# Residual rows of the output projection over five places, and two weight splits of the memory traced two steps later

## The chip, the cores and the metric

The kernel runs on one core of one Trainium2 chip. The metric is the device time in microseconds of one execution. A second kind of execution is taken by the hardware profiler, and all views of the profile below come from that one. The engines are TensorE (PE, with its weight loads shown apart as PEld), VectorE (DVE), ScalarE (ACT), GpSimd (POOL) and SyncE (SP), on whose queue all transfers of this kernel are issued.

## The reference

One inference step of one layer of a streaming encoder, for a prompt of 1024 frames and a sample of 64 frames that share the weights, in f32. Cut to what matters:

```python
h = rms_norm(xp, g_norm1)
qa, ka, va, qb, kb, vb, logf = in_proj(h, w_in, b_f, g_qa, g_ka, g_qb, g_kb)
oa = chunk_band_attn_prompt(qa, ka, va, rel_bias)   # 8 heads, 64-frame chunks, 8 chunks back
ob = forget_attn_prompt(qb, kb, vb, logf)           # 8 heads, causal, with forget bias
xp = xp + concat([oa, ob]) @ w_o                    # output projection and residual
mk, mv = mem_kv(mem_prompt, g_mem, w_mkv, g_mk)     # keys and values of 256 memory tokens
xp = xp + mem_attend(rms_norm(xp, g_norm2), mk, mv, w_mq, g_mq, w_mo)
xp = xp + conv_ffn(rms_norm(xp, g_norm3), zeros, w_up, w_conv, b_conv, w_down)
```

The sample goes through the same with cached keys and values. The outputs are both streams and the new keys, values, forget logits and conv states.

## The kernel before, in words

Every f32 product is made of three products of a high and a low part (`SPLIT = ((0, 0), (0, 1), (1, 0))`): an operand `raw` is split into `hi`, its rounded copy, made by ScalarE, and `lo = raw - hi`, made by VectorE or GpSimd. Activations are kept transposed, in 8 tiles of 128 features by 1088 frames (1024 of the prompt and 64 of the sample). The frames are worked on in three chunks of 384, 384 and 320 columns (`CHUNKS`).

The stages in order of time: projection and attention by head pairs (up to about 600 us in the profile), the memory's keys and values together with the sample's attention (to about 700), the output projection (to about 815), the memory's attention, and the feed-forward part.

The program is traced as Python. A planner then orders each engine's instructions when the program is compiled. Where the code wants an order kept it says so, as with `tc.keep_in_program_order(mm)` for the first matmul of the memory's keys. So the place in the trace of the program ranks an instruction, and the order in which it runs can differ. Waits between engines, and for a tile's place to be free, are put in by the framework: a tile tag with `bufs=n` has n places in turn.

*Around the splits.* After the last head pair is projected, its attention remains, and runs in four steps, `LEFT = (0, 0, 0, 15)`: each step traces the pieces of attention that are due (`substeps()`), and the number says how many pieces of the memory's product (`line`) are woven in. An attention piece goes through the bias (POOL, L485, with the causal mask L486), the score matmuls into the one bank S (L499), the masked maximum (DVE, L502), the exponential (ACT, L504), the scaling by the sum (L507 and L509), transposes into the banks PT (L539), their split into `pth` (ACT, L540) and `ptl` (DVE, L541), the value sum into the one bank O (L554), and its end: a copy `otmp` (ACT, L563) and an add into `mix` (DVE, L564).

The memory's weights come in 8 slices n of 256 columns. Each slice has two loads `mwraw` (`load_wm`, L661, two places) and four splits (`split_wm`, y = 0 to 3, two for each load): a cast `mwhi` on ACT (L668) and a subtraction `mwlo` (L669), on GpSimd for even y and on VectorE for odd y. Slice 0 has its splits y = 0 and 1 traced ahead of the four steps and y = 2 and 3 in the first pieces of `line`, in the fourth step. `load_mem` loads the memory tokens and splits them (`mhi` on ACT, L265, `mlo` on DVE, L266). The memory's matmuls are L679.

*The output projection.* `project` goes through 24 products (feature tile m, chunk c). For each it loads the residual chunk from `xT` (L1066) into the first half of a row tile, adds the product to it into the second half (DVE, L1073), stores that to `x1d` (L1074), and makes from it the next operand (`hhi`, ACT, L1076; `hlo`, DVE, L1077) and its square (ACT, L1079 or L1082), which GpSimd adds to one accumulator for each chunk (L1083). `after_o` reduces the accumulators over the features on PE (L1098). The row tile is the tag `qhi`, which has two places; `qlo` has two and `pth`, `ptl` and `sq` one each:

```python
BUFS = {"qhi": 2, "qlo": 2, "kvraw": 2, "s": 3}
```

The same tags serve the memory's attention afterwards: `qhi`, `qlo` and `sq` in `Mem.query`, `pth` and `ptl` in `Mem.turn`. The products go to two banks `PT` for the third and fourth and to two banks `pj` for the others; w_o's parts come through `Stream` (loads `raw`, L911; `hi`, ACT, L919; `lo`, POOL, L920).

## Time and profile before

| | |
|---|---|
| timed runs | 1780.97, 1782.76, 1785.41 us; median 1782.76 |
| profiled execution, its own time | 1788.58 us |
| its span, first to last instruction | 1786.6 us |
| mean granted TensorE clock | 0.988 |
| PE busy | 1717.5 us, 96% |
| DVE, ACT, POOL busy | 1210.5, 941.2, 647.3 us |
| DMA | 199.87 MB, mean 112 GB/s |

Times in the views are microseconds from the span's start. A row of a timeline gives the start, the duration, engine, line, operation, output and inputs with shapes, how many instructions are merged in it, and in brackets how long the engine stood idle before and what ended that. A row of waits gives the total, the number and the longest. A row by stretches gives the stretch, its length, the busy time and number of instructions of each engine, the granted clock as a share of the full one, the busy share of the DMA engines and GB/s.

### The profile page before, as it was taken

The page shows a single profiled execution, that of the slowest core. Times are in us where ns is not written, and L with a number is a line of the kernel's source. Part 1 is how long each engine was busy: PE and PEld are TensorE (multiplying, and loading weights), DVE is VectorE, ACT ScalarE, POOL GpSimd, SP SyncE. Part 2 cuts the span into 40 slices and gives each one's busy share as a digit, 9 for nine tenths or more (in the row PEclk, how much of TensorE's full clock was granted, in tenths as well). Part 3 has the DMA queues.
Part 4 walks back from the last instruction along what each step waited for, and adds up shares of the span by engine and source line. Part 5 has one row for each costly group of instructions (what it writes and reads, how often), then busy time and mean ns, then how long its engine had stood idle before and what let it go on. Part 6 is the DMA issues. An engine that isn't in the chain of part 4 may idle for free.

```text
span 1786.6 us, 33930 instructions
## 1 busy us (share of the span) xinstructions
PE 1717.5 (96%) x12432; PEld 1668.3 (93%) x12432; DVE 1210.5 (68%) x2643; ACT 941.2 (53%) x2058; POOL 647.3 (36%) x931
## 2 busy tenths in 40 slices
PE   7898999999998898999999999999999999999999
PEld 6888999999997777999999999999999999999999
DVE  5768667677677686433444369877777777649986
ACT  6756667677677577433555456434333333434432
POOL 4556667778777443453443612100000000000000
PEclk8999999999999999999999999999999999999999
DMA  7322222122112777541111563222222222693332
GB/s 251 91 62 64 60 77 78 49 74 76 51 56 83 216 252 219 165 143 56 54 54 60 151 214 104 79 75 77 79 85 85 85 73 73 216 346 130 118 104 88
DMA packets 134391, 199.87 MB, mean 112 GB/s; under 512 B 20984, under 2 KB 74360, under 8 KB 134224
## 3 DMA queue, kind: packets, MB, share of 16 engines
q1 hardware_dynamic: 134224, 197.70, 35.0%
q8 instruction: 98, 1.61, 0.4%
q14 instruction: 69, 0.57, 0.1%
HBM read 155.35 MB, written 45.44 MB: 112 GB/s over the span
## 4 chain that ended last, share of the span: by engine, by line
PE 46%; DVE 4%; issue 2%; ACT 1%; POOL 1%; DMA 1%; SPq 0%; DVEq 0%; ACTq 0%; POOLq 0%
PE W L1449 24%; PE W L1773 11%; PE pj L937 7%; PE S L1192 1%; PE tq L1228 1%; PE O L1228 1%; POOL lo L920 1%; DVE f L1314 0%; PE PT L1215 0%; DMA f<-x2d 0%; DVE lo L920 0%; DMA h<-ad 0%; PE O L1192 0%; ACT hi L1313 0%; DVE qhi L1301 0%
## 5 line engine op out<-in xcount | busy, mean ns | idle before, releaser
L299 PE MATMUL pj<-whi,xhi 128*128 128x384 f32 (+1 forms) x512 | 195.8, 382 | 2.7 <-DVE flog L314 1.6
L299 PE MATMUL pj<-wlo,xhi 128*128 128x384 f32 (+1 forms) x512 | 177.0, 346 | 4.3 <-POOL wlo L123 4.3
L299 PE MATMUL pj<-whi,xlo 128*128 128x384 f32 (+1 forms) x512 | 175.9, 344 | 0.7 <-DVE xlo L131 0.7
L1555 POOL COPY s<-gp 128x2 f32<-128x2 f32 x22 | 15.8, 720 | 335.8 <-DVE gp L1554 335.8
L1449 PE MATMUL W<-h,hi 128*128 128x272 f32 x704 | 134.4, 288 | 1.4 <-ACT qlo L1585 1.4
L504 ACT ACTIVATE s<-s,mx 128x640 f32<-128x640 f32 (+7 forms) x128 | 94.4, 737 | 77.4 <-DVE mx L502 76.5
L1773 PE MATMUL W<-f,hi 128*128 128x272 f32 x672 | 127.1, 287 | 0.1
L541 DVE TENSOR_TENSOR ptl<-PT,pth 128x512 fp32r<-128x512 f32 (+2 forms) x192 | 99.4, 522 | 37.5 <-ACT pth L540 35.3
L1449 PEld LDWEIGHTS W<-h,hi 128*128 128x128 f32 x704 | 110.8, 188 | 1.6 <-ACT qlo L1585 1.6
L540 ACT CAST pth<-PT 128x512 fp32r<-128x512 f32 (+2 forms) x192 | 84.7, 449 | 41.7 <-PE PT L539 39.9
L1773 PEld LDWEIGHTS W<-f,hi 128*128 128x128 f32 x672 | 105.3, 188 | 0.4 <-DVE f L1520 0.4
L299 PEld LDWEIGHTS pj<-wlo,xhi 128*128 128x128 f32 x512 | 99.5, 194 | 5.9 <-POOL wlo L123 5.9
L299 PEld LDWEIGHTS pj<-whi,xhi 128*128 128x128 f32 x512 | 99.4, 194 | 4.3 <-DVE flog L314 1.9
L1449 PE MATMUL W<-h,lo 128*128 128x272 f32 x352 | 101.8, 289 | 0.0
L299 PEld LDWEIGHTS pj<-whi,xlo 128*128 128x128 f32 x512 | 98.3, 192 | 1.4 <-DVE xlo L131 1.2
L1773 PE MATMUL W<-f,lo 128*128 128x272 f32 x336 | 96.7, 288 | 0.0
L539 PE MATMUL PT<-ident,s 128*128 128x128 f32 x528 | 89.9, 277 | 6.9 <-DVE ptl L541 5.4
L1313 ACT CAST hi<-raw 128x512 fp32r<-128x512 f32 x68 | 42.2, 621 | 98.6 <-PE W L1449 59.2
L499 PE MATMUL S<-kh,q 128*128 128x256 f32 (+1 forms) x304 | 77.8, 281 | 13.5 <-DVE mx L502 13.5
L937 PE MATMUL pj<-a,hi 128*128 128x384 f32 (+1 forms) x352 | 89.3, 337 | 0.2 <-DMA mraw<-mixd 0.2
L507 POOL TENSOR_SCALAR s<-s,ssum 128x640 f32<-128x640 f32 (+6 forms) x96 | 70.8, 738 | 47.9 <-DVE ssum L505 34.3
L554 PE MATMUL O<-pth,v 128*128 128x256 f32 (+1 forms) x304 | 76.5, 277 | 8.5 <-DVE mix L564 7.7
(538 smaller groups left out, 6037.6 us busy)
## 6 DMA issues: line engine op xcount, KB each, us to landing
raw<-in_w_down_dram SPq DMA_DIRECT2D x45, 256.0 KB, 2.8
wraw<-in_w_dram SPq DMA_DIRECT2D x56, 192.0 KB, 2.5
raw<-in_w_up_dram SPq DMA_DIRECT2D x41, 256.0 KB, 2.8
h<-ad SPq DMA_DIRECT2D x32, 272.0 KB, 5.5
mwraw<-in_w_mkv_dram SPq DMA_DIRECT2D x16, 512.0 KB, 6.1
raw<-in_w_mo_dram SPq DMA_DIRECT2D x32, 256.0 KB, 3.2
kvraw<-in_w_down_dram SPq DMA_DIRECT2D x32, 256.0 KB, 3.0
ad<-t SPq DMA_DIRECT2D x22, 272.0 KB, 2.2
```

Source lines behind the costliest of these rows:

```text
L299: pe.matmul(pj[:, :nw], x2[a][:, k, t * P:(t + 1) * P], wt[k][b][:, :nw], start=n == 0, stop=n == 3 * KT - 1)
L499: pe.matmul(sp[:, a:a + (k1 - k0) * P], q, kk[:, h, src], start=m == 0, stop=m == 1)
L504: act.activation(s[:, :n], s[:, :n], ACT.Exp, bias=mx, scale=-1.0, accum_out=sm)
L507: pool.tensor_scalar(s[:, :n], s[:, :n], sm, 1.0, op0=ALU.mult, op1=ALU.mult)
L539: pe.transpose(pt[:, b - ch[0]], self.s[j][:, (b - w0) * P:(b - w0 + 1) * P], ident)
L540: act.copy(hi[:, f:f + n, j], pt[:, f:f + n])
L541: dve.tensor_tensor(lo[:, f:f + n, j], pt[:, f:f + n], f32(hi[:, f:f + n, j]), op=ALU.subtract)
L554: pe.matmul(op[:, cols], groups[p, b // 2].v[:, b % 2, h].rearrange("p a d -> p (a d)"), pt[:, x, cols], start=b == self.full[0] and m == ...
L937: pe.matmul(out()[:, :cn], w[a][:, k % 4], x[b][k][:, c0:c0 + cn], start=k == 0 and n == 0, stop=k == KT - 1 and n == 2)
L1313: act.copy(hi, t)
L1449: pe.matmul(w[:, z, :Q], a(p, j), rights[j][b][:, z * Q:z * Q + Q], start=fresh and begin and j == 0 and x == 0, stop=final and end and j ...
L1773: pe.matmul(ws[m][:, z, :Q], la[p][:, m * P:(m + 1) * P], ra[b][:, z * Q:z * Q + Q], start=first and y == 0 and what in opening, stop=fina ...
```

## The change

Two edits. The two splits y = 0 and 1 of the memory's slice 0 (the first two quarters of its weights) are traced at the start of the third step in place of ahead of the first. And the residual row of product n takes its place from a list of five in turn: `qhi`, `pth`, `qhi`, `ptl`, `sq`, of which `qhi` has two places.

```diff
     load_mem(0)
     load_wm(0, 1)
     load_mem(1)
-    split_wm(0, 0)
-    split_wm(0, 1)
-    for n in LEFT:
+    for x, n in enumerate(LEFT):
+        if x == 2:
+            split_wm(0, 0)
+            split_wm(0, 1)
         step(n, substeps())
...
         for n, (m, c) in enumerate(order):
             c0, cn = CHUNKS[c]
-            xr = row("qhi", 768)
+            xr = row(("qhi", "pth", "qhi", "ptl", "sq")[n % 5], 768)
             xr, xo = xr[:, 0:cn], xr[:, 384:384 + cn]
             if firsts and n == 0:
                 xr = early_x
```

## The prediction

> **What bounds the kernel now.** I read the page's head first, then the busy time by stretches around the two places that the diff touches.

> ```profile
> PE 1717.5 (96%) x12432; PEld 1668.3 (93%) x12432; DVE 1210.5 (68%) x2643; ACT 941.2 (53%) x2058; POOL 647.3 (36%) x931
> ```

> TensorE works 96% of the span, so time is won only where TensorE waits or runs slowly. The second view says how the touched places stand in that.

> ```profile
> 565.00:575.00 10.00, 6.02 (x48) 5.52 (x46) 6.83 (x17) 7.66 (x20) 4.10 (x8) 0.95 0.65 210
> 575.00:585.00 10.00, 4.73 (x19) 3.88 (x19) 8.38 (x12) 7.22 (x15) 7.27 (x10) 0.54 0.73 246
> 585.00:600.00 15.00, 11.82 (x85) 10.02 (x86) 10.88 (x23) 10.49 (x19) 8.54 (x10) 1.00 0.72 204
> ...
> 720.00:740.00 20.00, 20.00 (x122) 19.57 (x121) 7.26 (x21) 7.59 (x18) 6.87 (x6) 1.00 0.55 167
> ```

> The columns after the stretch are its length, then busy time and instructions of PE, PEld, DVE, ACT and POOL, then the granted clock. From 565 to 600, where the attention of the last head pair ends and the memory's weights come in, PE is idle for 4.0 + 5.3 + 3.2 = 12.5 us, and has half a clock in the middle. The output projection, from 720 on, has PE busy without a hole. These are the places of the two halves of the change.

> **The moved splits.** The list of PE's waits between 560 and 705 us has this at its head:

> ```profile
> PE O L554 <- DVE mix L564: 7.7, 1, 7.7
> ```

> The value sum of the attention needs the one bank named O, which is free when ScalarE has copied it (otmp, L563) and VectorE has added it (mix, L564). Here is what stood around these two: ScalarE, VectorE, GpSimd, the DMA queue (with the landing times of the raw weights), and PE:

> ```profile
> 571.77 1.29 ACT L265 ACTIVATE mhi<-s,gcol 128x256 fp32r<-128x256 f32 x3
> 574.31 1.14 ACT L668 CAST mwhi<-mwraw 128x512 fp32r<-128x512 f32 x2 [1.24 <-DMA mwraw<-in_w_mkv_dram]
> 575.47 0.37 ACT L563 COPY otmp<-O 64x256 f32<-64x256 f32 x1
> 575.86 1.07 ACT L540 CAST pth<-PT 128x512 fp32r<-128x512 f32 x2
> 576.82 1.15 ACT L668 CAST mwhi<-mwraw 128x512 fp32r<-128x512 f32 x2
> ```
> ```profile
> 575.48 3.00 DVE L669 TENSOR_TENSOR mwlo<-mwraw,mwhi 128x512 fp32r<-128x512 f32 x1 [1.89 <-ACT mwhi L668]
> 578.51 0.42 DVE L564 TENSOR_TENSOR mix<-O,otmp 64x256 f32<-64x256 f32 x1
> 578.85 1.07 DVE L502 CUSTOM_DVE_ANT_0 s<-S,s 128x896 f32<-128x896 f32 x1
> ...
> 585.58 1.29 DVE L669 TENSOR_TENSOR mwlo<-mwraw,mwhi 128x512 fp32r<-128x512 f32 x1
> ...
> 587.87 0.83 DVE L669 TENSOR_TENSOR mwlo<-mwraw,mwhi 128x512 fp32r<-128x512 f32 x1
> ```
> ```profile
> 575.69 1.01 POOL L485 TENSOR_SCALAR s<-bias,ctok 128x896 f32<-128x896 f32 x1
> 576.66 1.26 POOL L669 TENSOR_TENSOR mwlo<-mwraw,mwhi 128x512 fp32r<-128x512 f32 x1
> 577.89 0.74 POOL L486 TENSOR_SCALAR_AFFINE_SELECT s<-s 128x128 f32<-128x128 f32 x1
> ...
> 583.57 0.29 POOL L486 TENSOR_SCALAR_AFFINE_SELECT s<-s 128x128 f32<-128x128 f32 x1
> ```
> ```profile
> 578.54 0.34 SPq L661 DMA_DIRECT2D mwraw<-in_w_mkv_dram  x1
> ```
> ```profile
> DMA to landing us min/median/max: 3.6/6.1/8.8
> ```
> ```profile
> 579.07 0.55 PE L554 MATMUL O<-pth,v 128*128 128x256 f32 x1 [7.69 <-DVE mix L564]
> 579.98 0.58 PE L499 MATMUL S<-kh,q 128*128 128x256 f32 x1 [0.36 <-DVE mx L502]
> ```

> The change moves two splits, y0 and y1: two casts on ScalarE (574.31), y0's subtraction on GpSimd (576.66) and y1's on VectorE (575.48). They issue no DMA themselves, but the end of y1 frees a raw buffer, and the next load on the SP queue stands right behind it (575.48 + 3.00 = 578.48, issue at 578.54); that load moves too. Without the two casts, otmp goes when the three mhi end, at 571.77 + 1.29 = 573.06; with 0.37 for it, 0.42 for mix and the 0.14 from mix's end to the matmul as now (578.93 to 579.07), the O matmul runs at 574.0, 5.1 us earlier.

> That is not yet 5.1 us of time. PE executes in order, and behind that matmul stand the scores (579.98), which wait for the one S bank, read by the maximum L502 (578.85). L502 needs the bias from GpSimd: L485 ends at 575.69 + 1.01 = 576.70, and the masking L486, no longer behind y0, takes 0.29 in its short row: 577.0. So L502 starts at 577.0 in place of 578.85: **1.85 us gained** on the path. The rest of the 5.1 us turns into a new wait, for L502.

> What is late next: the moved work must go somewhere. ScalarE has 10 - 7.22 = 2.8 us idle in the stretch 575 to 585 for the casts (1.14), GpSimd 2.7 us for y0 (1.26); both are hidden there and would cost those durations if L504's exponentials or the biases stood behind them. On VectorE I expect y1 beside y3, the split of lowest rank, which now runs at 585.58 between two L502 whose results free the S bank. VectorE does not idle there (no idle mark in either row), and I charge the row of y3, **1.29 us**; the ends are 0.83 and 3.00, and 1.29 is the nearest in place. But then the next raw load goes out near 586.9 and lands at least 3.6 us later, past 590, so that the subtraction of the following quarter, at 587.87, leaves the full part too: **0.83 us back**. Sum of this half: -1.85 + 1.29 - 0.83 = **-1.39 us**; its ends are -5.1 (nothing else holds the path) and +0.3 (-1.85 + 3.00 - 0.83).

> [...]

> **The rotated rows.** Before, each residual chunk is loaded, added to and stored from one of two places, so load n+2 waits until store n has landed. Five places take that wait away. No instruction is added or removed: 23 loads and 24 stores stay on SP, the loads earlier, and the weights' loads behind them on that queue are held up less. What do the waits cost now? From VectorE three adds of the stage, then PE where it comes nearest to waiting, then PE's waits from 705 to 830 us:

> ```profile
> 737.00 0.49 DVE L1073 TENSOR_TENSOR qhi<-PT,qhi 128x320 f32<-128x320 f32 x1 [3.71 <-DMA qhi<-in_xT_dram]
> ...
> 739.48 0.56 DVE L1073 TENSOR_TENSOR qhi<-pj,qhi 128x384 f32<-128x384 f32 x1 [0.80 <-DMA qhi<-in_xT_dram]
> ...
> 804.30 0.56 DVE L1073 TENSOR_TENSOR qhi<-pj,qhi 128x384 f32<-128x384 f32 x1 [2.00 <-PE pj L937]
> ```
> ```profile
> 740.21 0.56 PE L937 MATMUL pj<-a,hi 128*128 128x384 f32 x2
> ```
> ```profile
> PE pj L937 <- POOL lo L920: 0.7, 1, 0.7
> PE PT L1098 <- POOL kSl L1083: 0.6, 1, 0.6
> ```

> The early adds wait up to 3.71 us for a load; the late ones wait for PE itself. Neither stops PE: two banks PT and two pj take the products meanwhile. It is close: the product that starts at 740.21 reuses the bank of the add of 739.48, which ends at 740.04. So the waits are hidden, narrowly, and taking them away gives **0**; without that cover each would cost PE its own length. The wait of 0.6 at the stage's end follows a sum behind a PE product, not a load. The ends are -0.6, should earlier sums clear GpSimd, and +0.7, PE's one wait for a weight part here, should a burst of loads put the weights behind it. The borrowed places (pth, ptl, sq) are next used by the memory queries, after the last stores, so nothing queues there.

> The sum is -1.39 + 0 = -1.4 us. The profiled execution took 1788.58 us (span 1786.6 and 2.0 around it), 5.8 us above the median 1782.76 of the three timed runs; I take the difference off both: 1787.2 profiled, **1781.4** as a median. A measurement of this kernel tells about 0.3% (5.3 us) from no change, so this is no change.

> **The rivals.**

> *The whole wait goes (faster).* A planner makes the order on each engine; with PE free at 574.0 it may bring L485 forward and the scores with it. Then the full 5.1 us come, and if the clock of 0.54, which follows the wait of 7.69 us, stays up, the 4.73 us of PE work beside it shrink by 4.73 x 0.46 = 2.2. Time 1782.76 - 5.1 - 2.2 = 1775.5; without the clock 1777.7, with the 0.6 as well 1774.9. For it: the wait addressed is the longest of PE's here. Against it: L485 starts at 575.69 now with no split in front of it. Chance 0.25. [...]

> *Nothing moves (no change).* The planner issued the casts of y2 and y3 at 576.82, although they are traced later than the moved ones will be. It could do so with y0 and y1, ahead of otmp as now. Then 1782.8. Against it: PE is idle from 579.07 - 7.69 = 571.4, so the O products were done by then, otmp was ready and yet stood behind the casts: rank decided. Chance 0.20.

> *The weights come late (slower).* y1 gets behind the whole attention. The memory's matmuls wait for it, and the next raw load too:

> ```profile
> 600.30 0.33 PE L679 MATMUL pj<-mwhi,mhi 128*128 128x256 f32 x1
> ...
> 607.05 0.28 PE L679 MATMUL pj<-mwhi,mhi 128*128 128x256 f32 x1
> ```

> The matmul at 600.30 is the first to need y1 (six go before it), that at 607.05 the first of the next quarter. From y1 starting at 600.30 on, this decides: it ends 3.00 later, the load lands 8.8 after that, cast and subtraction take 0.57 and 1.29: 614.0, or 6.9 us behind 607.05. Time 1789.7; with 1.29 for y1 and a landing of 6.1 it is 2.5 us and 1785.3. Against it: y1 outranks all of the third and fourth steps. Chance 0.12.

> **How the numbers follow.** My forecast has 0.43, the rivals 0.25, 0.20 and 0.12. Its own range is 1777.1 (-5.1 - 0.6) to 1783.8 (+0.3 + 0.7). With the rivals it is 1774 to 1788.5, which leaves out the far end of the last. Faster by over 0.3% (below 1777.4) are most of the first rival and a little of the forecast's edge, 0.28; slower (above 1788.1) most of the last, 0.11; the other 0.61 is no change.

> **What would show it.** In the changed profile: otmp ahead of the first mwhi on ScalarE; PE's wait for mix far below 7.7 us, and a new one for L502 of about 3 us; L502 near 577; a mwlo of VectorE more near 585; the raw load of 578.54 near 587. In the output projection: early adds that no longer wait for loads, PE still without a hole, the wait for GpSimd still there. I am wrong if the S bank did not hold the path (then a gain near 5), if the clock stays up, or if PE waits for mwlo at the first memory matmuls.

## The result, and the profile after

| | before | changed |
|---|---|---|
| median of the timed runs, 12 each | 1784.05 us | 1787.31 us |
| lowest and highest | 1780.97, 1785.41 | 1784.67, 1793.54 |
| mean granted TensorE clock in the profile | 0.988 | 0.986 |
| profiled execution, its own time | 1788.58 us | 1786.59 us |

The ratio is 1.0024, with a 95% interval of 1.0016 to 1.0031: the change makes the kernel slower, by 0.24% or some 4 us. The forecast was 1.4 us faster. On the median that the forecast started from, the ratio gives 1782.76 x 1.0024 = 1787.0, so 5.6 us above the 1781.4.

The two profiled executions show the opposite sign, 1788.58 against 1786.59, and this has to be cleared first. Here are two stretches that lie ahead of everything the diff touches, before and then changed (a row has the length, the busy time of PE, PEld, DVE, ACT and POOL, the granted clock, and the DMA):

```profile
20.00:120.00 100.00, 85.00 (x507) 79.48 (x507) 68.82 (x215) 64.82 (x181) 51.80 (x71) 0.90 0.37 113
120.00:560.00 440.00, 427.68 (x2951) 411.13 (x2950) 311.18 (x855) 300.12 (x774) 320.51 (x531) 1.00 0.22 63
```
```profile
20.00:120.00 100.00, 84.64 (x518) 78.89 (x518) 70.43 (x219) 67.03 (x188) 52.09 (x72) 0.93 0.40 118
120.00:560.00 440.00, 427.72 (x2953) 411.23 (x2953) 311.82 (x856) 300.73 (x776) 319.90 (x531) 1.00 0.21 63
```

The first 120 us, which are the same in both programs, happened to get a clock of 0.90 and 0.93. The slow windows of this kernel run at half the clock (rows at 0.50 and 0.51 stand at the end of this text), so the time at half clock is length x (1 - clock) x 2: 20 us against 14. That is luck of one execution, and it must be taken out: all later times are counted from the last matmul of the projection, which is the same instruction in both. Before, then changed, that matmul and the first and last of the memory:

```profile
567.19 0.33 PE L347 MATMUL pj<-wlo,xs 128*128 128x384 f32 x1
...
598.69 0.28 PE L679 MATMUL pj<-mwhi,mhi 128*128 128x256 f32 x1
...
699.47 0.28 PE L679 MATMUL pj<-mwhi,mlo 128*128 128x256 f32 x1
```
```profile
565.15 0.34 PE L347 MATMUL pj<-wlo,xs 128*128 128x384 f32 x1
...
596.39 0.28 PE L679 MATMUL pj<-mwhi,mhi 128*128 128x256 f32 x1
...
698.06 0.28 PE L679 MATMUL pj<-mwhi,mlo 128*128 128x256 f32 x1
```

From the projection to the first memory matmul it is 31.50 before and 31.24 after, and from there to the last 100.78 and 101.67. One pair of profiles doesn't carry such differences. The second profile of before (e4 below) has these three matmuls at

```profile
565.35 0.33 PE L347 MATMUL pj<-wlo,xs 128*128 128x384 f32 x1
...
596.69 0.28 PE L679 MATMUL pj<-mwhi,mhi 128*128 128x256 f32 x1
...
695.68 0.28 PE L679 MATMUL pj<-mwhi,mlo 128*128 128x256 f32 x1
```

which is 31.34 and 98.99, and the second of the changed kernel (e3) has 31.34 and 102.35. So the first stretch is level, and the second is 0.9 to 3.4 us longer, where two profiles of before alone differ by 1.8. From the last memory matmul to the first of the output projection both profiles of before have 11.08 us, those of the changed kernel 11.82 and 11.78. From the projection's end to the kernel's end the changed kernel is on average 2.1 us longer; the profiles don't place the rest of the 4.

The long stall that the change addresses is gone all the same. The head of PE's waits between 560 and 705 us, changed kernel:

```profile
PE O L554 <- ACT pth L540: 3.5, 2, 3.1
PE S L499 <- DVE mx L502: 2.7, 3, 1.8
PE PT L710 <- DVE kv L698: 2.2, 2, 2.0
PE pj L679 <- POOL mwlo L669: 2.1, 4, 0.6
PE PT L822 <- ACT s L808: 1.9, 1, 1.9
```

Instead of one wait of 7.7 us for mix there are 3.1 and 1.8, and two of about 2 in the memory's stage. What came of it shows by stretches, before and then changed:

```profile
570.00:590.00 20.00, 9.88 (x61) 8.32 (x60) 16.30 (x31) 14.79 (x32) 14.48 (x18) 0.74 0.69 229
590.00:700.00 110.00, 98.86 (x701) 86.25 (x701) 77.15 (x189) 71.60 (x178) 46.10 (x47) 1.00 0.72 225
```
```profile
570.00:590.00 20.00, 13.80 (x59) 11.67 (x60) 15.77 (x30) 14.06 (x30) 12.46 (x17) 0.57 0.66 222
590.00:700.00 110.00, 100.14 (x702) 88.66 (x700) 77.74 (x186) 72.14 (x181) 44.93 (x48) 0.97 0.73 224
```

TensorE does about as many matmuls (61 and 59), and is busy 3.9 us longer with them, at a clock of 0.57 in place of 0.74: 17 us of half clock in place of 10. (In the changed profile the matmuls of L679 follow one another every 0.12 us at the clock of 1.00 near 602 us, and every 0.21 us at that of 0.51 near 608.) In the memory's stage the clock is 0.97 where it was 1.00, so 6.6 us of half clock where there was none. Both profiles of each kernel agree in this.

### The profile page after: what moved, and what is told of

Read it like the earlier page. It is cut to its first block, busy times and chain, and to the rows that moved or that the text cites. A ratio compares the mean times of both kernels' runs of the same rounds, so it can differ in the third digit from the quotient of the medians.

```text
span 1784.8 us, 33940 instructions
## 1 busy us (share of the span) xinstructions
PE 1720.3 (96%) x12432; PEld 1670.5 (94%) x12432; DVE 1212.5 (68%) x2643; ACT 942.2 (53%) x2058; POOL 644.2 (36%) x931
## 4 chain that ended last, share of the span: by engine, by line
PE 77%; DVE 8%; ACT 6%; issue 3%; POOL 3%; DMA 3%; SPq 0%; DVEq 0%; POOLq 0%; ACTq 0%
PE W L1450 25%; PE W L1774 13%; PE pj L938 12%; PE pj L299 11%; PE O L554 3%; PE S L499 2%; PE PT L539 2%; PE pj L679 1%; DVE s L502 1%; ACT s L504 1%; PE tq L326 1%; PE S L1193 1%; PE tq L1229 1%; PE O L1229 1%; POOL lo L921 1%
## 5 line engine op out<-in xcount | busy, mean ns | idle before, releaser
L504 ACT ACTIVATE s<-s,mx 128x640 f32<-128x640 f32 (+7 forms) x128 | 94.4, 737 | 76.7 <-DVE mx L502 76.0
L540 ACT CAST pth<-PT 128x512 fp32r<-128x512 f32 (+2 forms) x192 | 84.8, 449 | 42.8 <-PE PT L539 41.2
L499 PE MATMUL S<-kh,q 128*128 128x256 f32 (+1 forms) x304 | 78.4, 282 | 14.2 <-DVE mx L502 14.1
L539 PEld LDWEIGHTS PT<-ident,s 128*128 128x128 f32 x528 | 66.3, 142 | 17.0 <-DVE ptl L541 10.2
```

Of the source, the lines that this page charges most:

```text
L499: pe.matmul(sp[:, a:a + (k1 - k0) * P], q, kk[:, h, src], start=m == 0, stop=m == 1)
L504: act.activation(s[:, :n], s[:, :n], ACT.Exp, bias=mx, scale=-1.0, accum_out=sm)
L539: pe.transpose(pt[:, b - ch[0]], self.s[j][:, (b - w0) * P:(b - w0 + 1) * P], ident)
L540: act.copy(hi[:, f:f + n, j], pt[:, f:f + n])
```

## The experiments

**Which half.** Theory 1 puts the loss on the moved splits, theory 2 on the rotated rows. The four of this group ran on one chip, with the kernel before.

*e1*, the splits alone, and *e2*, the rows alone:

```diff
# e1: the changed kernel, but
-            xr = row(("qhi", "pth", "qhi", "ptl", "sq")[n % 5], 768)
+            xr = row("qhi", 768)
# e2: the kernel before, but
-            xr = row("qhi", 768)
+            xr = row(("qhi", "pth", "qhi", "ptl", "sq")[n % 5], 768)
```

> Only the splits are moved; the residual rows keep their two places. Theory 1 (the split move costs the time: it spreads TensorE's work over 572 to 590 us so that the clock stays at half for five windows in place of three, and brings the memory's weights later): this kernel alone is about 4.2 us slower than before (ratio 1.0024), the first memory matmul is as late as in the changed kernel. Theory 2 (the rotated rows cost it, in the output projection or behind it): this kernel is 0 to 1.5 us faster than before. Theory 3 (each half costs something): about 2 us slower.

> Only the residual rows rotate over five places; the splits stay where they were. Theory 1: 0 us against before (within 0.5 us). Theory 2: about 4.2 us slower, seen as new waits of TensorE behind 705 us. Theory 3: about 2 us slower.

*e3* and *e4* are the two kernels themselves.

> The changed kernel itself once more, on the same chip as the two halves: about 4.2 us slower than before by every theory, and a second profile of it. If the two halves add up, its ratio is the product of theirs. A clock at half from 572 to 589 again says that the long slow stretch belongs to the kernel and not to one execution.

> The kernel before itself, timed as though it were another: ratio 1.000; what it shows beside that is the scatter of this comparison, expected at 0.5 us or less. Its second profile tells whether the half clock lasts 10 us near 574 in every execution of before, and whether the two slow windows at the start, which made the first profile 4 us longer than the timed runs, are of the kernel or of that execution.

| | median | ratio to before, 95% |
|---|---|---|
| e1 splits alone | 1790.27 | 1.0037 (1.0024 to 1.0051) |
| e2 rows alone | 1782.92 | 0.9998 (0.9989 to 1.0007) |
| e3 changed again | 1786.68 | 1.0023 (1.0012 to 1.0034) |
| e4 before again | 1784.27 | 1.0006 (0.9997 to 1.0015) |

The splits cost, the rows alone do nothing: theory 1 as to the place. The halves don't add up, though: by the medians the splits alone are 3.6 us slower than both together (the intervals overlap). Where this can come from, the output projection of e1 shows: an add of VectorE, the PE row behind it, and the stretch around them, and then that stretch of the changed kernel.

```profile
738.45 0.56 DVE L1074 TENSOR_TENSOR qhi<-pj,qhi 128x384 f32<-128x384 f32 x1 [2.61 <-DMA qhi<-in_xT_dram]
```
```profile
739.16 0.59 PE L938 MATMUL pj<-a,hi 128*128 128x384 f32 x2 [1.87 <-DVE qhi L1074]
```
```profile
735.00:750.00 15.00, 13.13 (x70) 12.90 (x69) 5.45 (x8) 4.62 (x10) 5.63 (x5) 0.89 0.46 151
```
```profile
735.00:750.00 15.00, 15.00 (x94) 15.00 (x94) 5.93 (x9) 5.76 (x11) 8.49 (x8) 1.00 0.66 199
```

Without the rotation the add waits 2.61 us for its residual row, TensorE 1.87 us for the add, and then it runs a window at half clock (0.89 of 15 us is 3.3 us of it). With the rotation TensorE has no hole there, and the output projection takes 103.8 and 103.2 us from its first matmul to its last in the changed kernel's two profiles, where e1 has 107.1. So the rows do hide a stall, but one that comes up only with the splits moved (or, as e10 below shows, with the order that the move brings); before, at 104.2 and 104.1, had it narrowly covered.

Both profiles of before (e4 is the second) show the 10 us of half clock behind the wait of 7.7 and 7.6 us, and both of the changed kernel show 17 us behind the shorter ones: that belongs to the kernels. The half clock in the first 120 us differs in all of them.

**Filling the stalls, first try.** If the half clock carries the loss, matmuls that nobody reads, in the stalls, should bring the time back. They are traced ahead of a step of the attention, and the planner puts them where it sees TensorE idle. The edits, shortened:

```diff
     for x, n in enumerate(LEFT):
...
+        if x == 3:                        # e5, e8: 45; e7 (rows alone): 25 at x == 1
+            tq = bank("tq")
+            for _ in range(45):
+                pe.matmul(tq[:, :256], kh[:, 0, :P], kh[:, 0], start=True, stop=True)
         step(n, substeps())
# e8 has 16 more ahead of the first memory key
# e6, no extra matmuls: y1 on GpSimd
-        (dve if y % 2 else pool).tensor_tensor(lo, raw, f32(hi), op=ALU.subtract)
+        (dve if y % 2 and n + y != 1 else pool).tensor_tensor(lo, raw, f32(hi), op=ALU.subtract)
```

> The changed kernel with 45 extra matmuls (128x256, 0.12 us each at full clock, result unused) that fill TensorE's waits between 566 and 582 us. Theory 1 (the half clock gave the split move's gain back): the half clock from 570 to 587 shrinks to 3.4 us or less, the scores and transposes behind the third maximum take 1.05 and 1.15 us again in place of 1.85 and 1.5, the first memory matmul comes 30.2 us after the last projection matmul in place of 31.3, and the kernel is 1 us or more faster than the changed one. Rival (VectorE holds the path there, with the two mwlo of 2.3 us between two maxima): the clock rises and the first memory matmul still comes at 31.3.

> The changed kernel with the subtraction of y1 on GpSimd in place of VectorE. Theory 1: VectorE's stretch in front of the third maximum (2.3 us for two mwlo) loses 1.3 us or more, that maximum starts about 0.7 us earlier (17.7 in place of 18.45 after the last projection matmul), but the half clock still takes most of it; the first memory matmul 0 to 0.4 us earlier. Rival (VectorE holds the path): the first memory matmul 0.7 to 1.3 us earlier and the kernel as much faster than the changed one.

> The rotated rows, the splits where they were, and 25 extra matmuls (128x256, result unused) in TensorE's wait of 7.6 us. The half clock there lasted 10.2 us. Theory 1: the half clock gets one or two windows shorter, and the first memory matmul stays at 31.3 us after the last projection matmul, since the path of before went through the bias on GpSimd and not through TensorE; time as with the rows alone (1783 us). The rival of the prediction (the half clock costs 2.2 us there): 1 to 2 us faster.

> As the first of these four, and 16 more extra matmuls in the wait of 2.0 us for the first memory key (kv), behind which both profiles of the changed kernel show 3.4 us of half clock at 41 us after the last projection matmul. Theory 1: that slow window goes too, and the time from the first to the last memory matmul is about 1.7 us shorter than in the changed kernel (100.0 in place of 101.7 to 102.4); in all 2 to 3 us faster than the changed kernel, so level with before. Rival (the order of the memory's stage itself is worse): the slow window goes and the stage still takes 101 us or more.

| | median | ratio to before, 95% |
|---|---|---|
| e5 | 1788.02 | 1.0026 (1.0015 to 1.0036) |
| e6 | 1790.00 | 1.0034 (1.0022 to 1.0046) |
| e7 | 1782.88 | 0.9993 (0.9983 to 1.0002) |
| e8 | 1792.37 | 1.0042 (1.0030 to 1.0054) |

Three of the four don't say what they were built for. In e5 the clock rises to 1.00 from 570 to 590 us (0.57 in the changed kernel), and the first memory matmul comes at 21.1 us after the last of the projection and not at 30.2 (last projection matmul at 565.71):

```profile
586.80 0.36 PE L679 MATMUL pj<-mwhi,mhi 128*128 128x256 f32 x1
...
699.25 0.28 PE L679 MATMUL pj<-mwhi,mlo 128*128 128x256 f32 x1
```

That isn't speed: with the extra matmuls in its plan, the planner put memory matmuls ahead of attention work, and the stage to the last one takes 112.45 us in place of 101.67. e8 does the same. In e6 the third maximum is at 17.7 us after the projection, as expected, and the first memory matmul at 31.2, but the memory's stage has 10 us of half clock and another order again. e7 is the clean one: TensorE's order is that of the rows alone, the half clock in the attention is one window shorter (6.8 us), and the first memory matmul stays at 31.5. That window, at least, held nothing up.

The miss gave the next theory. TensorE's order differs between before and the changed kernel, though no matmul was touched by the diff: of its 12383 matmuls, 340 stand in another place. 30 of them are in the attention, where the first batch of 8 scores has gone behind 3 transposes and 7 value sums, and 310 in the memory's stage.

**Holding TensorE's order.** The order of one kernel is imposed on the other with order-only edges (no wait for an end) between neighbours (shortened):

```diff
+    for x, y in zip(PE_ORDER, PE_ORDER[1:]):   # 834 places, from the first that differs to the last
+        tc.add_manual_dep(traced[y].ins, traced[x].ins.name, ORDER_ONLY)
```

e9 is the changed kernel with the order of before, e10 the kernel before (no split moved, rows not rotated) with the order of the changed one, e11 and e12 the changed kernel with the order of before in the memory's stage alone and in the attention alone.

> The changed kernel with TensorE's whole order (340 of 12383 places differ between the two kernels) held to that of before; splits and rows as changed. Theory 2 (not the moved splits but the order that the planner then gave TensorE costs the time): level with before or up to 1.5 us faster (1782 to 1784 us). Theory 1 (the clock, from the shorter stalls): also about level, since the long wait for O comes back as the order does. Rival (the moved splits themselves, on ScalarE, VectorE, GpSimd and the loads): still 3 us slower than before.

> The kernel before, splits and rows untouched, with TensorE's order held to that of the changed kernel. Theory 2: 3 us slower than before (1787 us) without any split moved. Rival (the moved splits themselves): within 1 us of before.

> The changed kernel with TensorE's own new order up to the first memory matmul (30 places) and the order of before from there on (310 places). Theory 2, memory stage: level with before or faster, although the half clock near 570 to 587 stays. Theory 1 (the clock there): still 2 us or more slower than before.

> The other half: the changed kernel with the order of before up to the first memory matmul, and its own new order from there on. Theory 2, memory stage: as slow as the changed kernel (1787 us), although the half clock near 570 is back at 10 us. Theory 1: level with before.

| | median | ratio to before, 95% |
|---|---|---|
| e9 changed, order of before | 1783.95 | 1.0002 (0.9994 to 1.0011) |
| e10 before, new order | 1790.54 | 1.0044 (1.0032 to 1.0056) |
| e11 changed, memory's stage as before | 1785.44 | 1.0012 (1.0004 to 1.0021) |
| e12 changed, attention as before | 1784.94 | 1.0010 (1.0001 to 1.0018) |

With TensorE's order of before the loss is gone although the splits are traced late (e9), and its interval ends below those of the changed kernel. With the new order a loss comes without any split moved (e10). So a new order of TensorE, with what follows from it, is enough for a loss, and late splits with the old order don't bring it. More than that the two runs don't show, since the planner ordered the other four engines anew around the held order. In e9 the first mwlo of VectorE starts 10.9 us after the projection, in the changed kernel 16.1, before 8.3: so the moved splits weren't tested in the place that they have in the changed kernel. And the wait for O, which theory 1 expected back, doesn't come back (3.2 us the longest).

e10's loss does not lie where the changed kernel's does. From the projection to the first memory matmul it takes 34.53 us, 3 us more than any profile of before or of the changed kernel:

```profile
562.50 0.33 PE L50 MATMUL pj<-wlo,xs 128*128 128x384 f32 x1
...
597.03 0.28 PE L50 MATMUL pj<-mwhi,mhi 128*128 128x256 f32 x1
```

In the output projection, where it has no rotation either, it meets the stall of e1 (106.6 us). PE's waits of e10 there (all matmuls pass through one helper line):

```profile
PE pj L50 <- DVE qhi L1086: 2.1, 1, 2.1
```

By their medians each half of the order carries about half of the loss, which theory 2 of this group (all in the memory's stage) had not expected. The intervals of e11 and e12 reach from near nothing to near the whole, and the profiles don't follow the halves: e11, with the order of before in the memory's stage, still takes 101.67 us there, with 6.8 us of half clock, and e12, with the new one, 99.97 with 3.4.

e9 tells something on the clock: from 570 to 590 and 590 to 700 us,

```profile
570.00:590.00 20.00, 12.59 (x62) 11.60 (x62) 14.80 (x27) 13.99 (x27) 13.31 (x17) 0.59 0.64 215
590.00:700.00 110.00, 99.92 (x711) 87.27 (x709) 77.08 (x190) 72.68 (x183) 46.62 (x48) 1.00 0.73 225
```

it has as long a half clock in the attention as the changed kernel (0.59), but none in the memory's stage, and is level with before. Against a simple reading stands e2: level too, with 3.4 us of half clock in the memory's stage and 102.2 us for it.

**The clock or the order.** What remains is how the order costs time. e13 and e14 hold TensorE's order as the changed kernel has it and put extra matmuls into its stalls at fixed places; e15 and e16 do so with the rows alone. The edit, shortened:

```diff
+    def busy(x, out=None):       # at the places of FILL; e13: 20, 12, 14, 12; e14: 14, 12
+        tq = bank("tq") if out is None else out
+        extra = [pe.matmul(tq[:, :256], x[:, :P], x[:, :256], start=True, stop=True) for _ in range(n)]
```

> The changed kernel with its own order of TensorE held fast, and extra matmuls (128x256, result unused) in four of its stalls: 20 ahead of the value sum that waited 3.2 us, 12 ahead of the scores that waited 1.8, 14 ahead of the first transposed key (2.0), 12 ahead of the first sample transposes (1.8). Clock theory: the half clock from 570 to 589 and the two slow windows near 604 and 625 go, and the kernel is 2.5 to 4 us faster than the changed one, level with before (1.0000 to 1.0008). Order theory: the clock rises and the time stays within 1 us of the changed kernel (1.0018 to 1.0025).

> The same with the last two fillings only (14 and 12 matmuls, in the memory's stage). Clock theory: the 6.8 us of half clock in that stage go, the stage takes about 100 us in place of 102, the kernel is about 1.7 us faster than the changed one (1.0012 to 1.0015). Order theory: as the changed kernel (1.0018 to 1.0025).

> Rotated rows, splits and order as before, and 28 extra matmuls (3.4 us at full clock) in the stall of 4.0 us ahead of the output projection, behind which every profile shows 6.8 to 10.2 us of half clock. Clock theory: that half clock goes or shrinks to 3.4 us, and the kernel is 1.5 to 3.5 us faster than before (0.9980 to 0.9992). If the work there waits for something else (the weights' parts, the mix), no gain.

> As the one before this, and 50 more extra matmuls (6 us) in the stall of 7.6 us in the attention. The half clock of 10.2 us there goes. Since the path of before ran through the bias on GpSimd and the splits, and not through TensorE, I expect nothing more from it: within 1 us of the one before this. The prediction's price for that clock would make it 2.2 us faster.

| | median | ratio to before, 95% |
|---|---|---|
| e13 | 1795.24 | 1.0055 (1.0042 to 1.0068) |
| e14 | 1793.19 | 1.0047 (1.0034 to 1.0060) |
| e15 | 1784.42 | 0.9995 (0.9986 to 1.0005) |
| e16 | 1786.57 | 1.0008 (1.0000 to 1.0017) |

Inconclusive again. e13 and e14 are slower than either theory allowed. In e15 the half clock ahead of the output projection is gone (the mean clock of the timed runs is 0.9920, that of before beside it 0.9903), and nothing is gained; e16 still has 13.7 us of half clock in the attention, so it doesn't say what it was built for. The planner moved the other engines around the fillings; the longest wait of e14 in the memory's stage, where the changed kernel waits 2.2 us in all, is

```profile
PE PT L55 <- DVE kv L721: 8.1, 4, 4.7
```

So the last two hold the order of all five engines, from the last head pair to the end of the output projection, and the extra matmuls are meant to be all that is new: e17 in the changed kernel at the four stalls, e18 in the rows alone at the one ahead of the output projection. The edit, shortened:

```diff
+    for e, order in ORDERS.items():            # PE, ACT, DVE, POOL, SP
+        for x, y in zip(order, order[1:]):
+            tc.add_manual_dep(engines[e][y], engines[e][x].name, ORDER_ONLY)
```

> The changed kernel with the order of all five engines held to its own from the last head pair to the end of the output projection, and 20, 12, 14 and 12 extra matmuls in the four stalls (3.2, 1.8, 2.0 and 1.8 us). Clock theory: nearly no half clock from 570 to 690, the memory's stage takes about 100 us in place of 102, and the kernel is 2 to 4 us faster than the changed one (1.0000 to 1.0012). Order theory: the clock rises, TensorE idles as much longer, and the time stays within 1 us of the changed kernel (1.0018 to 1.0030).

> Rotated rows and splits as before, the order of all five engines held to that kernel's own, and 28 extra matmuls in the stall of 4.0 us ahead of the output projection. Clock theory: the 6.8 to 10.2 us of half clock there go, and the kernel is 1.5 to 3 us faster than before (0.9983 to 0.9992), which would beat both kernels. Otherwise level with the rows alone (0.9995 to 1.0002).

| | median | ratio to before, 95% |
|---|---|---|
| e17 | 1785.89 | 1.0008 (0.9999 to 1.0017) |
| e18 | 1782.10 | 0.9997 (0.9988 to 1.0006) |

e17, in the stretches shown above and at the first and last memory matmul (last projection matmul at 565.71):

```profile
570.00:590.00 20.00, 13.14 (x85) 11.30 (x84) 16.12 (x32) 14.11 (x30) 12.47 (x17) 0.91 0.64 226
590.00:700.00 110.00, 101.11 (x730) 89.33 (x728) 78.22 (x187) 72.32 (x182) 45.40 (x48) 1.00 0.72 224
```
```profile
597.00 0.28 PE L701 MATMUL pj<-mwhi,mhi 128*128 128x256 f32 x1
...
698.44 0.28 PE L701 MATMUL pj<-mwhi,mlo 128*128 128x256 f32 x1
```

The half clock is gone but for one window, and the kernel is at 1.0008 where the changed one is at 1.0023 and 1.0024: 0.15%, or 2.7 us, of the 4 are back, by work that computes nothing. That speaks for the clock as the carrier of the larger part. It is not shown: the intervals overlap (0.9999 to 1.0017 against 1.0016 to 1.0031 and 1.0012 to 1.0034), no run holds the five orders without the extra matmuls, and the profile, whose own time of 1787.81 is the second longest of this kernel's 11, has the first memory matmul at 31.29 and the stage at 101.44, both within 0.3 us of the changed kernel's first profile. What of the loss is clock and what is waits in the new order stays open in its sizes.

The timed runs show the half clock too. Their mean granted clock is 0.9868 for the changed kernel (e3), 0.9907 for before beside it, and 0.9922 for e17 (0.9904 for before beside that). 0.0039 less of 1784 us is 14 us more of half clock, as in the profiles. What such a difference goes with can be counted from executions of one and the same kernel, whose orders are fixed. Over the 296 timed runs of the changed kernel, of e1 to e18 and of before beside them, each taken against its own group's mean, an execution is 0.49 us longer for each us that the clock loses (time x (1 - clock)). At that rate the 7.0 us that e3 loses against before go with 3.4 us, of 4.1 measured. This is a correlation, since a longer wait may also have lowered the clock (waits of 2.0 and 1.9 us went ahead of half clock in the rows at the end of this text), and it fails where the order has waits of its own: 1.2 us of the 7.8 of e10, and e17, with a better clock than before, should be 1.6 us faster than it and is 1.4 slower.

In e18 the half clock ahead of the output projection goes, as these stretches of e2 and of e18 show:

```profile
705.00:720.00 15.00, 12.51 (x56) 10.74 (x57) 12.02 (x19) 11.05 (x24) 6.91 (x4) 0.77 0.68 219
```
```profile
705.00:720.00 15.00, 13.01 (x70) 10.88 (x68) 11.97 (x22) 10.37 (x27) 7.30 (x4) 1.00 0.59 189
```

The expected 1.5 to 3 us don't come, as in e15: that half clock can go without any gain that these runs could show. No kernel of this study beats before by more than its interval; e2, e7 and e18 are level with it and 4 to 5 us faster than the changed kernel.

## Why the prediction was wrong, step by step

*The stall and the S bank: right.* ScalarE, VectorE and GpSimd of the changed kernel around the place:

```profile
570.94 0.37 ACT L563 COPY otmp<-O 64x256 f32<-64x256 f32 x1
...
572.30 1.15 ACT L668 CAST mwhi<-mwraw 128x512 fp32r<-128x512 f32 x2
```
```profile
574.94 1.09 DVE L502 CUSTOM_DVE_ANT_0 s<-S,s 128x896 f32<-128x896 f32 x1 [1.69 <-POOL s L486]
...
576.49 3.03 DVE L266 SCALAR_TENSOR_TENSOR mlo<-s,gcol,mhi 128x256 fp32r<-128x256 f32 x4
579.44 1.21 DVE L502 CUSTOM_DVE_ANT_0 s<-S,s 128x1024 f32<-128x1024 f32 x1
...
581.22 2.29 DVE L669 TENSOR_TENSOR mwlo<-mwraw,mwhi 128x512 fp32r<-128x512 f32 x2
...
583.50 1.06 DVE L502 CUSTOM_DVE_ANT_0 s<-S,s 128x896 f32<-128x896 f32 x1
...
587.17 1.23 DVE L502 CUSTOM_DVE_ANT_0 s<-S,s 128x1024 f32<-128x1024 f32 x1 [1.79 <-PE S L499]
```
```profile
576.12 2.27 POOL L485 TENSOR_SCALAR s<-bias,ctok 128x1024 f32<-128x1024 f32 x2
```

The copy otmp goes ahead of the first mwhi, and the first maximum, which waits for the masking L486 as the prediction had it, starts 9.79 us after the projection, where it stood at 578.85 - 567.19 = 11.66: 1.87 gained against a forecast of 1.85.

*Where it went: the sizes wrong, one term missing.* The three maxima of before that follow the one shown in the prediction:

```profile
583.89 1.22 DVE L502 CUSTOM_DVE_ANT_0 s<-S,s 128x1024 f32<-128x1024 f32 x1 [1.11 <-POOL s L486]
...
586.87 1.06 DVE L502 CUSTOM_DVE_ANT_0 s<-S,s 128x896 f32<-128x896 f32 x1
...
589.79 1.22 DVE L502 CUSTOM_DVE_ANT_0 s<-S,s 128x1024 f32<-128x1024 f32 x1
```

So the four of before start at 11.66, 16.70, 19.68 and 22.60 us after the projection, those of the changed kernel at 9.79, 14.29, 18.35 and 22.02. The gain is 1.87, 2.41, 1.33 and 0.58, and 0.26 at the first memory matmul, where the second profiles of the two kernels differ by nothing. The forecast had -1.85 + 1.29 - 0.83, which is 1.39 kept. Between the second and the third maximum two subtractions come together, as forecast for y1 and y3, but take 2.29 us, and the third starts right behind them: 1.08 lost of that gain. Between the third and the fourth stands what the sum lacked: VectorE waits 1.79 us for eight scores that TensorE makes at half clock (0.50 from 583 to 587 us). The sum charged nothing for the clock; the 0.83 that the next quarter's subtraction was to give back (its row now runs at 593.03) is used up there. The load that was to go out near 587 goes out at 583.05 + 2.04 = 585.1 on the time of before.

*The step that failed.* The prediction moved four instructions on ScalarE, GpSimd and VectorE and a load, and left TensorE's order as it was; only the faster rival let the planner bring scores forward, and it put them back instead. The text of the program ranks the instructions, so a split traced later can change the planner's order on engines that have no part in the move; here it changed 340 places of TensorE. With that order held to the old one the kernel is level with before (e9, 1.0002, 0.9994 to 1.0011), which leaves no room for the 5.1 us of the rival, and the 1.39 us of the sum (0.9992) lie just outside. With the new order alone a kernel is slower (e10), though for a good part in other stages. So the step that failed is the fixed order, and with it the clock at no charge. By which part of the new order the 4 us are lost, and how much of them goes by the clock, stays open.

The slower rival, "the weights come late", did not come: the changed kernel waits 2.1 us in all for GpSimd's mwlo, with 0.6 the longest, and before 2.0. The sign came from a mechanism that was not among the cases, and the measured time lies beyond the 1783.8 that the forecast gave as its own upper end.

*The rotated rows: right in the order of before, wrong in the new one.* In e2 they are worth 0 (0.9998), as forecast, and the adds wait less for loads, though not as little as forecast: VectorE stands 20.9 us in all behind them in this stage before, 4.1 in e2 and 8.2 in the changed kernel, there up to 2.3 at once. The second add of the stage, in e1 and in the changed kernel:

```profile
727.27 0.56 DVE L1074 TENSOR_TENSOR qhi<-pj,qhi 128x384 f32<-128x384 f32 x1 [3.05 <-DMA qhi<-in_xT_dram]
```
```profile
726.39 0.56 DVE L1074 TENSOR_TENSOR pth<-pj,pth 128x384 f32<-128x384 f32 x1 [0.42 <-DMA pth<-in_xT_dram]
```

The prediction said that the cover is narrow and that without it each wait would cost its own length. The other half of the change took the cover away (1.87 us of wait and a slow window in e1), and the prediction priced the halves one by one.

## What to carry to other kernels

Where a planner orders the instructions, an edit's cost isn't the moved work alone: compare the whole order of every engine before and after, and price an order that changes where nothing was moved as an unknown; here new orders cost 0.1% to 0.5%. To test a cause in such a kernel, hold the orders of all engines first, and run that once with nothing else added: with some of them free, extra matmuls measured the planner's next order and not the clock. Count what a stall's removal does to the clock as well: here one wait of 7.7 us went with 10 us of half clock, several of 2 to 3 us with 24.

## What the runs showed of the hardware that was not expected

Stalls of 2.0 and 1.9 us went ahead of a slow window each. The changed kernel in stretches of one window each, around these waits:

```profile
602.90:606.30 3.40, 1.38 (x12) 1.20 (x12) 3.33 (x4) 0.91 (x4) 3.40 (x6) 0.99 0.15 45
606.30:609.70 3.40, 3.40 (x18) 3.40 (x17) 2.80 (x8) 0.79 (x3) 2.50 (x5) 0.51 0.47 121
...
623.30:626.70 3.40, 1.53 (x13) 1.23 (x12) 2.94 (x12) 2.98 (x8) 1.11 (x2) 1.00 1.01 315
626.70:630.10 3.40, 3.40 (x12) 2.90 (x11) 2.83 (x7) 2.96 (x9) 0.21 (x1) 0.50 0.94 293
```

Four mlo on VectorE take 3.03 us at 576.49, beside a GpSimd row of 2.27 us that starts at 576.12. Before, GpSimd had no row beside the same four:

```profile
580.46 1.66 DVE L266 SCALAR_TENSOR_TENSOR mlo<-s,gcol,mhi 128x256 fp32r<-128x256 f32 x4
```

The row of 3.00 us in the prediction, at 575.48, stands beside GpSimd rows too (575.69 and 576.66). But so do the rows of 1.29 us at 585.58 and of 0.83 us at 587.87, with the same operation and size: GpSimd has rows at 585.21 (1.13 us) and at 587.04 (1.12 us). What makes VectorE's rows longer was not shown.
